# A step between two layers with tokens on the partitions, first sums of squares on TensorE, and last rows set among spilled pairs

## The chip, the cores and the metric

The kernel runs on one core of one Trainium2 chip. The metric is the time of one execution in microseconds on the device. The kernel before has a median of 2876.93 us over 3 runs (2876.14 to 2879.42). One execution was profiled; it took 2871.39 us by the same clock, and its trace spans 2869.6 us.

## The reference

A trunk of two layers works on two streams of 256 tokens with 1024 features each: the latent `x` and a context `ctx`. Each layer is a group of four token mixers and then an expert network (PEER). Cut to what matters here:

```python
for l in range(DEPTH):                     # DEPTH = 2
    last = l == DEPTH - 1
    sh1, sc1, g1, sh2, sc2, g2 = _modulation(c, w_mod[l], b_mod[l])       # silu(c) @ w_mod + b_mod
    sh1c, sc1c, g1c, sh2c, sc2c, g2c = _modulation(c_ctx, w_mod[l], b_mod[l])
    hx = _rmsnorm(x, norm_mix[l]) * (1 + sc1) + sh1
    hc = _rmsnorm(ctx, norm_mix[l]) * (1 + sc1c) + sh1c
    y, yc = _mixers(hx, hc, w_in[l], ..., not last)     # one input projection, four mixers, w_out
    x = x + g1 * y
    hx2 = _rmsnorm(x, norm_ffn[l]) * (1 + sc2) + sh2
    if last:
        x = x + g2 * _peer(hx2, ...)
    else:
        ctx = ctx + g1c * yc
        hc2 = _rmsnorm(ctx, norm_ffn[l]) * (1 + sc2c) + sh2c
        f = _peer(jnp.concatenate([hc2, hx2], axis=1), ...)
        ctx = ctx + g2c * f[:, :C]                      # C = 256 tokens of context
        x = x + g2 * f[:, C:]
return _rmsnorm(x, final_norm)
```

`_peer` takes for each token and each of 8 heads the 16 best of 128 x 128 experts, and adds `gate * gelu(h . u[i]) * v[i]` over them. `_rmsnorm` divides by the root of the mean square over the 1024 features.

## The kernel before

**Layout.** The streams lie in one tile `xT` of 128 partitions x 8 x 512: feature k*128+p of a token on partition p, the tokens on the free axis, first the 256 of the context (stream s = 0), then the 256 of x (s = 1). Features on the partitions are what a matmul wants that sums over features; a sum of squares over features then takes a matmul with a matrix of ones, and a gate per feature is a scalar per partition.

**Arithmetic.** Each fp32 operand of a large matmul is split into a high and a low part of a faster type (`hH` and `hL`, `wH` and `wL`, `vH` and `vL`, `ah` and `al`), and three products are summed: high x high, high x low, low x high. The splits run on ACT (high, L211) and on DVE or POOL (low, L215).

**Order of the work.** (1) The start: silu of c, its rows of 128 x 512 by four groups of matmuls (L284, copied by ACT at L286), the two modulation rows of layer 0, half by matrix products on PE (`mod_first`, L311 and L315), half by dot products on DVE (`mod_rows`, L296), and meanwhile the sums of squares of both streams: ACT squares each of 8 feature blocks (L339, L342), POOL adds them (L344), and two matmuls with ones bring the sum to all partitions (L347, L348). `norm_mod` (L360 to L364) turns xT into `hH` and `hL`. (2) The mixers of layer 0: the input projection in slabs of 128 columns (L224), then the mixers. (3) PEER of layer 0: scores over all experts (u phase), then the values (v phase) in pairs of expert blocks: `pa`, three token tiles of PSUM accumulators, gathers `ah`/`al` x `vH`/`vL` (L1312). Tile 0, the first 128 tokens of the context, is instead summed from single gathered rows by DVE and POOL, in the generator `gathered`, which runs in between the pairs; at its end it transposes its sum back (L1072) and adds it to xT (`resid`, L375). (4) The step between the layers: after the last pair the accumulators are copied (L1335, L1337), transposed to features (L1344), gated and added to xT (L375), squared and summed (`sumsq`), and `norm_mod` gives the `hH` and `hL` of layer 1. (5) Mixers of layer 1, (6) PEER of layer 1 for x alone. Its v phase begins with pairs whose scores are computed there and then, and ends with pairs that were spilled to memory earlier and are read back (`ga`). `finish_rows` (L1356, L1364) prepares what the end needs: the gate and the final gain as rows on all partitions, and x with tokens on the partitions; it stands ahead of the v phase. `finish` (L1378 to L1394) then gates, adds, normalises and stores.

**What sets the order.** In the v phase of layer 0 and in the step behind it the order on PE, DVE, ACT and POOL is that of the code. Elsewhere a scheduler orders the instructions within what the tiles' buffers allow. PSUM tiles with the name `S` go round in a small ring, so a group of transposes waits until the copy out of an earlier one is done.

Of the kernel before, what the change touches and what calls it, by code (L numbers as in the profile page):

```python
# [9 lines left out]
F32 = mybir.dt.float32  # L10
# [11 lines left out]
P = 128  # L22
D = 1024
KT = 8
# [47 lines left out]
GATED = (1, 4)  # L72
VALUES = (5, 0)
# [111 lines left out]
class Kernel:  # L185
# [149 lines left out]
    def sumsq(self, k, c, psp, tag, eng=None):  # L335
# [9 lines left out]
        else:  # L345
            ps = self.t(psp, [P, T], tag=tag)
            nc.tensor.matmul(ps[:, c], self.ones, self.sqsum[:, c], start=True, stop=False)  # L347
            nc.tensor.matmul(ps[:, c], self.ones, sq[:, c], start=False, stop=True)  # L348
            self.rstd_from(self.rstd[:, c], ps[:, c], D)
# [304 lines left out]
    def mixers(self, l, modt, tick=None, pre=()):  # L654
# [5 lines left out]
        with ExitStack() as es:  # L660
            fp = es.enter_context(tc.tile_pool(name=f"fp{l}", bufs=1))
            psp = es.enter_context(tc.tile_pool(name=f"ps{l}", bufs=2, space=PSUM))
            hx = self.norm_mod(0, modt, 1, 0, fp)
# [3 lines left out]
            def feat(name, ct, lo):  # L667
                w = slabs.pop(0) if slabs else self.in_slab(l, name, ct)
                b.nfeat += 1
                ps = self.proj(w, hx, lo, psp, last and b.nfeat <= 3)  # L670
                if tick:
                    ticks(1)
                return ps
# [182 lines left out]
            for piece in ORDERS[l]:  # L856
                name, _, d = piece.partition(":")
                locals()[name](*map(int, d))
            yT = (self.t(None, [P, KT, T], F32R, tag="hH"), self.t(None, [P, KT, T], F32R, tag="hL"))
# [134 lines left out]
    def gathered(self, l, gate, h2, idx, gates, gp, mods, modt):  # L994
# [74 lines left out]
        for q in range(2):  # L1069
            pt = self.t(self.gps[0], [P, 4, P], tag=self.gps[1])  # L1070
            for k in range(4):
                nc.tensor.transpose(pt[:, k, :], acc[:, (q * 4 + k) * P:(q * 4 + k) * P + P], self.ident)  # L1072
            for k in range(4):
                self.resid(q * 4 + k, pt[:, k, :], gate, 0, slice(0, P))
            yield

    def peer(self, l, mods, todo=()):
# [10 lines left out]
        with ExitStack() as es:  # L1088
# [122 lines left out]
            with ExitStack() as e2:  # L1211
# [11 lines left out]
                if last:  # L1223
                    rows = self.finish_rows(vp, psp, modt[5])
# [56 lines left out]
                for g, i in enumerate(order):  # L1281
                    ah, al, vs = b.ah, b.al, b.vs
                    left = len(order) - 1 - g
                    if left:
# [43 lines left out]
                self.norm_start()  # L1328
                f = {}
                for tau in taus:  # L1330
                    f[tau] = self.t(vp, [P, D], tag="vH", bufs=4)
                    for h in range(2):
                        dst = f[tau][:, h * 512:h * 512 + 512]
                        if h:
                            V.tensor_copy(dst, pacc[tau, h])  # L1335
                        else:
                            S.activation(dst, pacc[tau, h], AF.Copy)  # L1337
                for s, c in self.halves(dl):
                    for d in range(KT):
                        ps = self.t(psp, [P, T], tag="S")  # L1340
# [170 lines left out]
```

## Time and profile before

| | us |
|---|---|
| median of 3 runs | 2876.93 (2876.14 to 2879.42) |
| the profiled execution, its own time | 2871.39 |
| its span in the trace | 2869.6 |
| PE busy | 2705.5 (94% of the span) |
| DVE busy | 2048.3 (71%) |
| ACT busy | 1149.8 (40%) |
| POOL busy | 1098.5 (38%) |

PE is TensorE's matmul side, DVE VectorE, ACT ScalarE, POOL GpSimd, SP the engine that issues the DMAs. A share over the whole span is a mean over stages with different limits, so each stage is looked at by itself. Starts are in microseconds from the start of the span. The times of a sum are those of the profiled execution; 1.8 us of it lie outside the span.

### The profile page before, as it was taken

Reading aid. Unit: us, or ns where it says so; the run is one execution under the profiler, and the core shown is the slowest. Engines: PE = TensorE matmul, PEld = TensorE weight load, DVE = VectorE, ACT = ScalarE, POOL = GpSimd, SP = SyncE. Lnnn points to the kernel's source line nnn. Section 1 sums busy time; section 2 is a strip of 40 time slices with the busy share of each in tenths; the row PEclk is TensorE's granted clock in tenths of the full one; section 3 lists DMA queues with packets and bytes.
Section 4 is the critical chain, followed back from the end, with each engine's and each line's share of the span. In section 5 each row is a group of like instructions: output and inputs, shape, how many; then the busy total and the mean of one; then the engine's idle time right before and its main releaser. Section 6 shows DMA issues by size and latency. Waiting matters only on the chain. (4 is left out here: it accounts for less than half of the span.)

```text
span 2869.6 us, 41545 instructions
## 1 busy us (share of the span) xinstructions
PE 2705.5 (94%) x15778; PEld 2398.3 (84%) x15778; DVE 2048.3 (71%) x3608; ACT 1149.8 (40%) x1752; POOL 1098.5 (38%) x651
## 2 busy tenths in 40 slices
PE   7899999889999999999999998899889999999998
PEld 4677888789998888888888877688889998998776
DVE  6785778999677788898888877847982404555665
ACT  4433433235533333333333334434344545444443
POOL 3631134455145344344343313425656574440000
PEclk9898999989999999999999998999999999999999
DMA  6223423257789899999999952324557776667785
GB/s 238 67 81 111 128 89 121 93 171 269 282 294 321 304 327 329 323 340 338 346 328 342 378 195 67 110 89 149 158 183 240 234 257 205 213 207 255 268 273 186
DMA packets 265784, 639.25 MB, mean 223 GB/s; under 512 B 19184, under 2 KB 136688, under 8 KB 262768
## 3 DMA queue, kind: packets, MB, share of 16 engines
q1 hardware_dynamic: 228720, 502.36, 52.2%
q0 software_dynamic: 36864, 134.23, 12.8%
q8 instruction: 124, 2.03, 0.3%
q14 instruction: 76, 0.62, 0.1%
HBM read 574.39 MB, written 62.13 MB: 222 GB/s over the span
## 5 line engine op out<-in xcount | busy, mean ns | idle before, releaser
L215 POOL TENSOR_TENSOR wL<-wraw,wH 128x1024 fp32r<-128x1024 f32 x228 | 572.6, 2514 | 694.4 <-ACT wH L211 541.8
L224 PE MATMUL S<-hH,wL 128*128 128x384 f32 (+1 forms) x2048 | 606.4, 314 | 21.0 <-POOL wL L215 11.3
L224 PE MATMUL S<-hH,wH 128*128 128x384 f32 (+1 forms) x2048 | 606.3, 314 | 5.8 <-ACT wH L211 4.2
L211 ACT ACTIVATE wH<-wraw 128x1024 fp32r<-128x1024 f32 x320 | 337.1, 1054 | 335.0 <-DMA wraw<-in_uT_dram 297.9
L224 PEld LDWEIGHTS S<-hH,wL 128*128 128x128 f32 x2048 | 393.6, 192 | 32.1 <-DVE wL L215 17.9
L1312 PE MATMUL pa<-vH,al 128*128 128x512 f32 x1280 | 397.7, 391 | 8.3 <-DVE al L1263 7.9
L224 PEld LDWEIGHTS S<-hH,wH 128*128 128x128 f32 x2048 | 393.8, 192 | 11.2 <-ACT wH L211 6.8
L1312 PE MATMUL pa<-vL,ah 128*128 128x512 f32 x1280 | 396.9, 391 | 2.5 <-DVE vL L215 2.3
L1312 PE MATMUL pa<-vH,ah 128*128 128x512 f32 x1280 | 395.6, 390 | 2.0 <-ACT ah L1259 1.2
L215 DVE TENSOR_TENSOR vL<-wraw,vH 128x1024 fp32r<-128x1024 f32 x256 | 305.7, 1223 | 68.1 <-ACT vH L211 66.8
L224 PE MATMUL S<-hL,wH 128*128 128x384 f32 (+1 forms) x2048 | 347.5, 310 | 0.0
L211 ACT ACTIVATE vH<-wraw 128x1024 fp32r<-128x1024 f32 x256 | 263.9, 1054 | 188.6 <-PE pa L1312 158.0
L224 PEld LDWEIGHTS S<-hL,wH 128*128 128x128 f32 x2048 | 311.5, 190 | 0.0
L1013 POOL DMA_INDIRECT row<-in_v_dram,idx x128 | 190.4, 1487 | 293.4 <-DVE tok L1064 266.2
L1312 PEld LDWEIGHTS pa<-vH,al 128*128 128x128 f32 x1280 | 238.5, 188 | 65.2 <-DVE al L1263 16.4
L1013 POOL DMA_INDIRECT row<-in_u_dram,idx x128 | 182.2, 1424 | 279.0 <-DVE score L1046 237.5
L1312 PEld LDWEIGHTS pa<-vL,ah 128*128 128x128 f32 x1280 | 239.0, 188 | 57.2 <-DVE vL L215 8.0
L1312 PEld LDWEIGHTS pa<-vH,ah 128*128 128x128 f32 x1280 | 238.1, 188 | 48.1 <-ACT ah L1259 1.6
L1109 ACT ACTIVATE ga<-S 128x384 f32<-128x384 f32 (+1 forms) x256 | 111.1, 435 | 385.4 <-PE S L224 384.3
L224 PE MATMUL mm<-hH,wH 128*128 128x256 f32 (+1 forms) x776 | 256.1, 349 | 9.4 <-ACT hH L362 2.9
L224 PE MATMUL mm<-hH,wL 128*128 128x256 f32 (+1 forms) x776 | 251.4, 343 | 5.6 <-DVE wL L215 5.3
L215 DVE TENSOR_TENSOR wL<-wraw,wH 128x1024 fp32r<-128x1024 f32 x128 | 156.1, 1227 | 118.4 <-ACT wH L211 112.8
(340 smaller groups left out, 4048.8 us busy)
## 6 DMA issues: line engine op xcount, KB each, us to landing
wraw<-in_uT_dram SPq DMA_DIRECT2D x256, 512.0 KB
wraw<-in_v_dram SPq DMA_DIRECT2D x256, 512.0 KB
gd<-gst SPq DMA_DIRECT2D x20, 2048.0 KB
wraw<-in_w_in_dram SPq DMA_DIRECT2D x52, 512.0 KB
gt<-gd SPq DMA_DIRECT2D x32, 768.0 KB
row<-in_w_modT_dram SPq DMA_DIRECT2D x48, 512.0 KB
wraw<-in_w_modT_dram SPq DMA_DIRECT2D x32, 512.0 KB
wraw<-in_w_q_dram SPq DMA_DIRECT2D x32, 512.0 KB
```

Source lines behind the costliest of these rows:

```text
L211: nc.scalar.activation(h, w, AF.Copy)
L215: e.tensor_tensor(lo, w, h.bitcast(F32), op=ALU.subtract)
L224: nc.tensor.matmul(ps, x, y, start=start and m == 0, stop=stop and m == len(seq) - 1, skip_group_check=skip)
L1013: Gp.indirect_dma_start(out=x, out_offset=None, in_=rows[n], in_offset=bass.IndirectOffsetOnAxis(ap=idx[:, k:k + 1], axis=0))
L1109: self.gelu = S.activation(ga[:, e, :], ps, AF.Gelu_apprx_tanh)
L1312: nc.tensor.matmul(pacc[tau, h], (ah, ah, al)[m][:, e, tau * P:(tau + 1) * P], vs[e][m == 1][:, h * 512:h * 512 + 512], start=g == 0 and e ...
```

## The change

It has three parts.

**The step between the layers.** In the v phase of layer 0, six pairs before its end, a new function `token_rows` turns xT to tokens on the partitions (32 transposes, 8 copies) and makes the gates as rows on all partitions (16 matmuls with the identity, 4 copies). `gathered` no longer transposes its sum; it leaves it in `acc0`. After the last pair, `hand_over` gates and adds tile by tile with tokens on the partitions (`normed`), where the sum of squares of a token is a sum along the free axis; the normalised tile is transposed to features, modulated and split (`features`): first the tiles 0, 2, 3, then the features of x, then tile 1, then the features of the context. In layer 1 the first two slabs are projected for the columns of x first and then for those of the context. After the piece `d_out` of the mixers of layer 1 x is transposed back to features (16 transposes, 8 copies).

**The first sums of squares.** `sumsq_pe` takes the place of `sumsq`: 8 matmuls with ones, one for each feature block, sum the squares in PSUM; POOL's 6 adds are gone.

**The last step's rows.** `finish_rows` of layer 1 is called six pairs before the end of the v phase instead of ahead of it.

```diff
+ROWSAT = 6
...
+    def sumsq_pe(self, k, c, ps):
+
+        sq = self.t(None, [P, T], tag="t2")
+        self.nc.scalar.activation(sq[:, c], self.xT[:, k, c], AF.Square)
+        self.nc.tensor.matmul(ps[:, c], self.ones, sq[:, c], start=k == 0, stop=k == KT - 1)
+        if k == KT - 1:
             self.rstd_from(self.rstd[:, c], ps[:, c], D)
...
-            hx = self.norm_mod(0, modt, 1, 0, fp)
+            hx = self.hx if last else self.norm_mod(0, modt, 1, 0, fp)
...
             def feat(name, ct, lo):
+                if last and b.nfeat < 2:
+                    x = [(hx[0][:, k, C:], hx[1][:, k, C:]) for k in range(KT)]
+                    if b.nfeat == 0:
+                        b.two = [(self.in_slab(l, name, e), self.t(psp, [P, T], tag="mm", bufs=self.nmm)) for e in range(2)]
+                        for w, ps in b.two:
+                            self.mm3(ps[:, C:], [(w[0][:, k, :], w[1][:, k, :]) for k in range(KT)], x)
+                    w, ps = b.two[b.nfeat]
+                    b.nfeat += 1
+                    self.mm3(ps[:, :C], [(w[0][:, k, :], w[1][:, k, :]) for k in range(KT)],
+                             [(hx[0][:, k, :C], hx[1][:, k, :C]) for k in range(KT)])
...
+                if last and name == "d_out":
+                    for k in range(KT):
+                        ps = self.t(psp, [P, T], tag="tr")
+                        for c in (C, C + P):
+                            nc.tensor.transpose(ps[:, c:c + P], self.xT[:, k, c:c + P], self.ident)
+                        S.activation(self.xT[:, k, C:], ps[:, C:], AF.Copy)
...
-        for q in range(2):
-            pt = self.t(self.gps[0], [P, 4, P], tag=self.gps[1])
-            for k in range(4):
-                nc.tensor.transpose(pt[:, k, :], acc[:, (q * 4 + k) * P:(q * 4 + k) * P + P], self.ident)
-            for k in range(4):
-                self.resid(q * 4 + k, pt[:, k, :], gate, 0, slice(0, P))
-            yield
+        self.acc0 = acc
...
-                if last:
-                    rows = self.finish_rows(vp, psp, modt[5])
...
+                    if left == ROWSAT:
+                        rows = self.finish_rows(vp, psp, modt[5]) if last else self.token_rows(vp, psp, modt[5])
...
-                self.norm_start()
-                f = {}
-                for tau in taus:
...
+                self.hand_over(vp, pvp, taus, pacc, rows, mods[1])
+
+    def token_rows(self, pool, psp, gate):
+
+        nc = self.nc
+        for k in range(KT):
+            ps = self.t(psp, [P, 4, P], tag="S")
+            for tt in range(4):
+                nc.tensor.transpose(ps[:, tt, :], self.xT[:, k, tt * P:tt * P + P], self.ident)
+            nc.scalar.activation(self.xT[:, k, :], ps.rearrange("p t n -> p (t n)"), AF.Copy)
+        g = [[self.t(pool, [P, T], tag=tag, bufs=1) for tag in tags] for tags in (("grow0", "rstd"), ("grow1", "grow2"))]
+        for s in range(2):
+            for q in range(2):
+                ps = self.t(psp, [P, 4, P], tag="S")
+                for k in range(4):
+                    nc.tensor.matmul(ps[:, k, :], gate[q][:, k, s:s + 1].to_broadcast([P, P]), self.ident, start=True, stop=True)
+                nc.scalar.activation(g[s][q], ps.rearrange("p k n -> p (k n)"), AF.Copy)
+        return g
+
+    def hand_over(self, pool, pvp, taus, pacc, gates, modt):
...
+        def normed(tt, src, tag):
+            y = self.xT[:, :, tt * P:tt * P + P]
+            w[tt] = self.t(pool, [P, D], F32R, tag=tag, bufs=4).bitcast(F32)
+            wv = w[tt].rearrange("p (k n) -> p k n", n=P)
+            ss = self.t(pool, [P, 2], tag="ss")
+            for h in range(2):
+                c, q = slice(h * 512, h * 512 + 512), slice(h * 4, h * 4 + 4)
+                V.tensor_tensor(w[tt][:, c], src(h), gates[int(tt >= 2)][h], op=ALU.mult)
+                V.tensor_tensor(y[:, q], y[:, q], wv[:, q], op=ALU.add)
+                S.activation(wv[:, q], y[:, q], AF.Square, accum_out=ss[:, h:h + 1])
+            r = self.t(pool, [P, 1], tag="rs")
+            V.tensor_tensor(r, ss[:, 0:1], ss[:, 1:2], op=ALU.add)
+            self.rstd_from(r, r, D)
+            S.activation(wv[:, :4], y[:, :4], AF.Copy, scale=r)
+            V.tensor_scalar(wv[:, 4:], y[:, 4:], r, None, op0=ALU.mult)
+
+        def features(s, tags):
+            c = slice(s * C, s * C + C)
+            for k in range(KT):
+                if k % 2 == 0:
+                    ps = self.t(pvp, [P, 2, C], tag=tags[k // 2], bufs=1)
+                x = ps[:, k % 2, :]
+                for e in range(2):
+                    nc.tensor.transpose(x[:, e * P:e * P + P], w[s * 2 + e][:, k * P:k * P + P], self.ident)
+                sc, sh = [modt[m][k // 4][:, k % 4, s:s + 1] for m in (1, 0)]
+                if k % 2:
+                    S.activation(x, x, AF.Identity, scale=sc, bias=sh)
+                else:
+                    V.tensor_scalar(x, x, sc, sh, op0=ALU.mult, op1=ALU.add)
+                S.activation(H[:, k, c], x, AF.Copy)
+                V.tensor_tensor(L[:, k, c], x, H[:, k, c].bitcast(F32), op=ALU.subtract)
+
+        normed(0, lambda h: self.acc0[:, h * 512:h * 512 + 512], "vL")
+        for tau, tag in zip(taus[:2], ("vH", "vL")):
+            normed(tau + 1, lambda h: pacc[tau, h], tag)
+        features(1, [f"pa{tau}{h}" for tau in taus[:2] for h in range(2)])
+        normed(1, lambda h: pacc[0, h], "vH")
+        features(0, ["pa00", "pa01"] + [f"pa{taus[1]}{h}" for h in range(2)])
+        self.hx = H, L
...
-                    self.norm_start()
+                    self.rstd = self.t(None, [P, T], tag="rstd")
+                    acc = self.t(wmp, [P, T], tag="ss", bufs=1)
...
-                            self.sumsq(k, slice(0, T), wmp, "mm", nc.gpsimd)
+                            self.sumsq_pe(k, slice(0, T), acc)
```

Where the instructions stand now is shown at three places, on PE.

The first place is the end of the step, where layer 1's first projection starts. Before, the last transposes of the accumulators and the two sums stand ahead of the first projection matmul (`mm` is its PSUM tile, `hH` x `wH`):

```order
L1344 MATMUL S_14499<-small_59,vH_14404 128x128
L1344 MATMUL S_14505<-small_59,vH_14404 128x128
L347 MATMUL S_14510<-t_2801_14396,small_59 128x256
L348 MATMUL S_14510<-t_2836_14508,small_59 128x256
L224 MATMUL mm_14625<-hH_14553,wH_14621 128x256
L224 MATMUL mm_14625<-hH_14553,wL_14622 128x256
```

In the changed kernel (its own line numbers; `vL_14456` and `vH_14542` are the normalised tiles 0 and 1, the two of the context, and `small` holds the identity):

```order
L1401 MATMUL pa_2829_14531<-small_59,vH_14470 128x128
L1401 MATMUL pa_2829_14531<-small_59,vL_14484 128x128
L1401 MATMUL pa_2833_14556<-small_59,vL_14456 128x128
L1401 MATMUL pa_2833_14556<-small_59,vH_14542 128x128
...
L1401 MATMUL pa_2836_14589<-small_59,vL_14456 128x128
L1401 MATMUL pa_2836_14589<-small_59,vH_14542 128x128
L225 MATMUL mm_14656<-hH_14454,wH_14652 128x256
L225 MATMUL mm_14656<-hH_14454,wL_14653 128x256
```

All 16 transposes of the context, which read tile 1, stand ahead of the first projection matmul, which reads columns of x alone.

The second place is the v phase of layer 0, the pair with six left. Before, its matmuls followed those of the pair ahead without a break:

```order
L1312 MATMUL pa_1331_6761<-vL_13889,ah_13897 128x512
L1312 MATMUL pa_1332_6762<-vL_13889,ah_13897 128x512
L1312 MATMUL pa_1331_6761<-vH_13888,al_13898 128x512
L1312 MATMUL pa_1332_6762<-vH_13888,al_13898 128x512
L1312 MATMUL pa_1327_6757<-vH_13946,ah_13959 128x512
L1312 MATMUL pa_1328_6758<-vH_13946,ah_13959 128x512
```

In the changed kernel `token_rows` stands between two pairs (the last two of its eight groups of transposes are shown, and its four groups of gates):

```order
L1358 MATMUL S_14032<-small_59,xT_65 128x128 x4
L1358 MATMUL S_14038<-small_59,xT_65 128x128 x4
L1365 MATMUL S_14048<-small_59,mod_19_87 128x128 x4
L1365 MATMUL S_14054<-small_59,mod_20_88 128x128 x4
L1365 MATMUL S_14060<-small_59,mod_19_87 128x128 x4
L1365 MATMUL S_14066<-small_59,mod_20_88 128x128 x4
L1334 MATMUL pa_1327_6757<-vH_13946,ah_13959 128x512
L1334 MATMUL pa_1328_6758<-vH_13946,ah_13959 128x512
```

Twelve groups of four stand there, ahead of the next pair's first matmul.

The third place is `finish_rows` of layer 1. Before, between two score products (`S`, L224) at the start of the v phase:

```order
L224 MATMUL S_21358<-hL_16807,wH_21327 128x256 x8
L1356 MATMUL S_21400<-small_59,mod_31_99 128x128 x4
L1356 MATMUL S_21406<-small_59 128x128 x4
L1356 MATMUL S_21412<-small_59,mod_32_100 128x128 x4
L1356 MATMUL S_21418<-small_59 128x128 x4
L1364 MATMUL S_21425<-small_59,xT_65 128x128 x4
L1364 MATMUL S_21431<-small_59,xT_65 128x128 x4
L1364 MATMUL S_21437<-small_59,xT_65 128x128 x4
L1364 MATMUL S_21443<-small_59,xT_65 128x128 x4
L224 MATMUL S_21468<-hH_16806,wH_21451 128x256
```

In the changed kernel, among the products of the spilled pairs:

```order
L1334 MATMUL pa_4016_21460<-vH_25179,al_25188 128x512
L1426 MATMUL S_25254<-small_59,mod_31_99 128x128 x4
L1426 MATMUL S_25260<-small_59 128x128 x4
L1426 MATMUL S_25266<-small_59,mod_32_100 128x128 x4
L1426 MATMUL S_25272<-small_59 128x128 x4
L1434 MATMUL S_25279<-small_59,xT_65 128x128 x4
L1334 MATMUL pa_4013_21457<-vH_25218,ah_25230 128x512
L1434 MATMUL S_25285<-small_59,xT_65 128x128 x4
L1434 MATMUL S_25291<-small_59,xT_65 128x128 x4
L1334 MATMUL pa_4014_21458<-vH_25218,ah_25230 128x512
L1434 MATMUL S_25297<-small_59,xT_65 128x128 x4
L1334 MATMUL pa_4013_21457<-vL_25219,ah_25230 128x512
```

The same eight groups are there; the last three lie between products of the next pair.

## Rows read from the trace of the kernel before

**Rows 1.** Windows: length, busy PE, PEld, DVE, ACT, POOL; clock, DMA share, GB/s.

```profile
15.00:20.00 5.00, 0.00 (x0) 0.00 (x0) 4.93 (x5) 0.63 (x1) 4.84 (x3) 0.51 1.05 396
...
1600.00:1680.00 80.00, 80.00 (x355) 66.24 (x354) 66.94 (x65) 29.68 (x30) 19.07 (x12) 1.00 0.97 341
...
1712.00:1736.00 24.00, 11.18 (x32) 5.22 (x30) 17.33 (x45) 11.85 (x29) 1.36 (x1) 0.56 0.08 22
...
1860.00:1880.00 20.00, 19.80 (x128) 17.40 (x127) 9.46 (x25) 2.22 (x4) 1.15 (x1) 0.88 0.08 27
...
2374.00:2377.00 3.00, 3.00 (x14) 3.00 (x15) 0.00 (x0) 1.32 (x3) 1.74 (x1) 0.50 0.94 344
...
2380.00:2420.00 40.00, 39.93 (x268) 37.05 (x269) 18.39 (x13) 19.62 (x28) 18.97 (x8) 1.00 0.62 194
```

**Rows 2.** Timeline of the start: start, us, engine, line, tiles, count [idle before, releaser].

```profile
8.60 11.43 POOL L344 TENSOR_TENSOR t<-t,t 128x512 f32<-128x512 f32 x6 [4.35 <-ACT t L342]
...
18.95 2.16 DVE L296 CUSTOM_DVE_ANT_0 modj<-wmod,silu_rows,small 128x1024 bf16<-128x1024 f32 x1
...
22.48 1.28 DVE L296 CUSTOM_DVE_ANT_0 modj<-wmod,silu_rows,small 128x1024 bf16<-128x1024 f32 x1
...
20.08 2.08 PE L347 MATMUL mm<-t,small 128*128 128x512 f32 x2 [9.35 <-POOL t L344]
...
23.79 7.79 PE L311 MATMUL mm<-wf,silu_c 128*2 128x512 f32 x16
...
45.37 0.50 PE L224 MATMUL mm<-hH,wH 128*128 128x512 f32 x1 [0.25 <-DVE mod L317]
...
20.59 3.75 SPq L305 DMA_DIRECT2D wf<-in_w_first_dram  x2
```

**Rows 3.** Timeline of the step between the layers.

```profile
1701.18 2.98 DVE L1263 TENSOR_TENSOR al<-ga,ah 128x768 fp32r<-128x768 f32 x1 [0.36 <-ACT ah L1259]
...
1711.16 0.62 PE L1312 MATMUL pa<-vH,al 128*128 128x512 f32 x2
...
1724.95 0.91 ACT L362 ACTIVATE hH<-big,mod 128x256 fp32r<-128x256 f32 x2
...
1735.79 0.58 PE L224 MATMUL mm<-hH,wH 128*128 128x256 f32 x1 [0.56 <-ACT rstd L328]
...
1737.02 0.41 PE L224 MATMUL mm<-hH,wL 128*128 128x256 f32 x1
```

**Rows 4.** Timeline of `finish` at the end of layer 1, second tile.

```profile
2859.19 0.68 DVE L1378 TENSOR_TENSOR fo<-pa,grow 128x512 f32<-128x512 f32 x1
2859.91 0.69 DVE L1379 TENSOR_TENSOR xtok<-xtok,fo 128x512 f32<-128x512 f32 x1
...
2864.68 0.15 DVE L1386 TENSOR_TENSOR rs<-ss 128x1 f32<-128x1 f32 x1
2865.43 0.49 DVE L1394 TENSOR_SCALAR fo<-xtok,rs 128x512 f32<-128x512 f32 x1 [0.60 <-ACT rs L329]
...
2863.32 0.63 ACT L1381 ACTIVATE fo<-xtok 128x512 f32<-128x512 f32 x1 [1.96 <-DVE xtok L1379]
```

**Rows 5.** Timeline: transposes and rows by matmul, with their copies.

```profile
1682.81 0.60 PE L1072 MATMUL S<-small,tok 128*128 128x128 f32 x4
...
2369.70 1.05 PE L1356 MATMUL S<-small,mod 128*128 128x128 f32 x8
...
2373.86 2.08 PE L1356 MATMUL S<-small,mod 128*128 128x128 f32 x8 [2.21 <-ACT grow L1357]
...
2380.56 0.39 PE L224 MATMUL S<-hH,wH 128*128 128x256 f32 x1
...
2367.70 8.04 POOL L215 TENSOR_TENSOR wL<-wraw,wH 128x1024 fp32r<-128x1024 f32 x3 [4.18 <-ACT wH L211]
...
2379.42 1.09 ACT L1365 ACTIVATE xtok<-S 128x512 f32<-128x512 f32 x2
```

**Rows 6.** Waits of PE from 2600 to 2853 us: us in total, times, longest.

```profile
PE pa L1312 <- DVE al L1263: 6.9, 12, 1.0
```

More of the change, by code (lines that the diff above doesn't have):

```diff
@@ L348, in sumsq @@
             nc.tensor.matmul(ps[:, c], self.ones, sq[:, c], start=False, stop=True)
+            self.rstd_from(self.rstd[:, c], ps[:, c], D)
+    def sumsq_pe(self, k, c, ps):
[3 more added lines that the diff above has]
+        if k == KT - 1:
             self.rstd_from(self.rstd[:, c], ps[:, c], D)
@@ L662, in mixers @@
             psp = es.enter_context(tc.tile_pool(name=f"ps{l}", bufs=2, space=PSUM))
-            hx = self.norm_mod(0, modt, 1, 0, fp)
+            hx = self.hx if last else self.norm_mod(0, modt, 1, 0, fp)
             slabs = list(pre)
             def feat(name, ct, lo):
+                if last and b.nfeat < 2:
[8 more added lines that the diff above has]
+                             [(hx[0][:, k, :C], hx[1][:, k, :C]) for k in range(KT)])
+                    if tick:
+                        ticks(1)
+                    return ps
                 w = slabs.pop(0) if slabs else self.in_slab(l, name, ct)
@@ L1327, in peer @@
                     return
-                self.norm_start()
-                f = {}
-                for tau in taus:
[L1331 to L1340, printed above, removed]
-                        for tau in sorted(taus):
-                            at = dl + tau * P
-                            if c.start <= at < c.stop:
-                                nc.tensor.transpose(ps[:, at:at + P], f[tau][:, d * P:(d + 1) * P], self.ident)
-                        self.resid(d, ps, modt[5], s, c)
-                        self.sumsq(d, slice(s * C, s * C + C), psp, "S")
+                self.hand_over(vp, pvp, taus, pacc, rows, mods[1])
@@ new lines, in hand_over @@
+    def hand_over(self, pool, pvp, taus, pacc, gates, modt):
+        nc = self.nc
+        V, S = nc.vector, nc.scalar
+        H = self.t(None, [P, KT, T], F32R, tag="hH")
+        L = self.t(None, [P, KT, T], F32R, tag="hL")
+        w = {}
+        def normed(tt, src, tag):
[35 more added lines that the diff above has]
+        self.hx = H, L
```

## The prediction

> **What bounds the kernel now.** I read the table of busy shares first (DVE 71%, PE nearly full) and then asked, with windows, where PE isn't full, since only there can an edit off PE gain, and in the full stretches each instruction added to PE costs its own length. [...] In the v phase of layer 0 PE works 80.00 of 80 us, in the mixers of layer 1 19.80 of 20, and behind the start of layer 1's v phase 39.93 of 40 [rows 1]. At the start PE does nothing from 15 to 20 us, where DVE (4.93 of 5) and POOL (4.84) are full [rows 1]. [...] The timeline of each stretch then shows what the next matmul waits for.
>
> **Part 1, the first sums of squares.** Before, six adds of POOL hold the squares: 8.60 + 11.43 us = 20.03, and PE's sum starts at 20.08, its last releaser POOL L344 [rows 2]. `mod_first` follows at 23.79, and the first projection starts at 45.37 [rows 2]. Beside those adds the dot products on DVE take 2.16 us each, without them 1.28 [rows 2]. After: eight ones-matmuls of 128x512. The two of before took 2.08 at the lower clock [rows 2], so about 1.0 each while PE is warm, and PE comes warm from the silu rows. Eight follow their squares on ACT and on PE end near 17.4 instead of 23.8, so this chain gives 6.4. The weights of `mod_first` may be later than that: SP issues its next weight tiles only at 20.59 [rows 2], and by the order it waits there for the landing of this product's own two, so they may land as late as that and the first product may start anywhere between 17.4 and about 20.5 without a wait of its own coming last. That is a gain of 3.3 to 6.4, plus up to 0.7 if the first product, 7.79 long at a clock still rising [rows 2], runs warm throughout: 4 to 7. DVE, with 8 dot products at about 1.32 from start to start, is free near 21.4 instead of 25.1 and isn't last. I take the middle, **-5.5**. Everything behind shifts with it, PE being the limit from the first projection on.
>
> **Part 2, the step between the layers.** Before, the last product of the pairs ends at 1711.16 + 0.62 = 1711.8, the first projection starts at 1735.79: 24.0 us [rows 3]. After, DVE starts with tile 0 once its last `al` is done, 1701.18 + 2.98 = 1704.2 [rows 3], while PE still multiplies. A tile's chain has its rows in `finish`: two halves of a product (0.72 from start to start) and an add (0.69), 2.8; the square on ACT 0.63 and its sum about 0.2; from the add of the two sums to the scaling 0.75, the scaling 0.49 [rows 4]. Together 4.8 from tile to tile. Three tiles end at 1718.5. The features of x: per pair of blocks the modulation, two copies and two subtractions on DVE and ACT, each about 0.45 (the 256-column copies of L362 take 0.91 for two [rows 3]), some 2.0 a pair in the order written, 8.1 in all: 1726.6. Tile 1, 4.8: 1731.4, and about 0.8 until its ACT half is scaled.
>
> Then comes what the order on PE shows: the sixteen transposes of the context stand ahead of the first projection of x, so x's features, ready at 1727, wait for the context. Four transposes end 0.35 after their start when warm, the next product starting then (1682.81, 0.60 long with its drain [rows 5]), twice that when cold: 1.8 to 3.4 for sixteen. The first projection so starts between 1734 and 1735.6, against 1735.79. The first matmuls behind are cold in both (0.41 long at 1737.02 [rows 3]). I take **-1.5**. Both ends: if DVE's last `al`, 2.98 long for 768 columns, took what the 0.68 of a 512-column product [rows 4] makes by width, 1.0 (an estimate), 2 more are gained, and 0.5 more if the tiles overlap, so -4; if each tile costs 1 us more than in `finish` (four wide operands now pass through the strided xT, which no row shows), +3.
>
> What pays for it stands on a full PE. `token_rows`: eight groups of four transposes, each with a copy on ACT of 128x512 at 1.09 for two [rows 5], and a ring of few PSUM tiles: about 0.6 a group, 4.8. Four groups of gates: the first like it in `finish_rows` ends 0.9 to 1.05 after its start [rows 5], 3.8 for four. Together 8.6. The lower bound is PE's own time without a wait for copies, 8 x 0.35 + 4 x 0.9 = 6.4. The upper one is the rate at which `finish_rows` went: eight groups from 2369.70 to 2380.56, 10.86 [rows 5], so twelve take 16.3. There the second pair of gates was held 2.21 by the copy on ACT and ran at a clock of 0.50 (2.08 long instead of 1.05) [rows 1, 5]. In the v phase of layer 0 ACT works 29.68 of 80 us [rows 1], and its copies stand contiguous there, so I take the value near the lower end, 8.6. The transposes that fall away (L1072, two groups, 0.42 each with gaps) give 0.85 back: **+7.75**.
>
> The transposes of x back in layer 1: sixteen at 0.09 to 0.12, **+2**, on a PE busy 19.80 of 20 us [rows 1]; 1.5 if they fit with no gap, 4.9 if each pair waits for its copy (8 x 0.6).
>
> **Part 3, the last step's rows.** Removed: 10.86 from 2369.70 to 2380.56 [rows 5]. Not all comes back: the next score product reads a low part that POOL makes at 2367.70 + 8.04/3 = 2370.4, 0.7 behind the place, and the following ones go at POOL's rate of 2.68 a tile [rows 5], so 1 to 2 us of waits that the rows hid come out: 8 to 10.9, I take 9.4. Behind it PE is full (39.93 of 40) with a DMA share of 0.62 [rows 1], so the transfers can follow. Added: the same eight groups among the spilled pairs, ACT being free there: 4 x 0.95 + 4 x 0.55 = 6.0, at most 10.9 as before. PE has 6.9 us of waits for `al` in 253 us there [rows 6], about 1 in what is left of the pairs after the place, and that may absorb 1: 4.9. Net **-4.5**, from -2 to -6.5.
>
> **Sum.** -5.5 - 1.5 + 7.75 + 2 - 4.5 = -1.75 against the profiled execution's 2871.39: 2869.6. The median is 5.5 above the profiled execution, so about **2875** for the median after. A change within 0.2%, 5.75 us, can't be told from none.
>
> [...] In the stretch from 2374 to 2377, with PE busy 3.00 of 3.00 after a wait of 2.21, the granted clock was 0.50 [rows 1, 5]; it is a row with gates, not with transposes alone. [...]
>
> **Rivals.**
> First, the gains reach their bounds: no DMA holds `mod_first` (-7), the start of layer 1's v phase gives back all 10.9 (-6), and the short `al` starts the step earlier (-3.5). With 7.75 and 2 that is -6.75: 2870. For it speaks that all three are waits whose releasers are seen to go; against it the late issue at 20.59 and the 2.68 a tile on POOL. Add a `token_rows` at its lower bound and it is 2868.
>
> Second, slower: the clock falls inside `token_rows`. PE alternates there with ACT's copies for some 5 us; from the point at which the level falls before the gates, four groups of gates cost 1.9 instead of 0.95, +3.8, and the first products of the next pair go at half rate for as long as it lasts, some 2 to 3 us lost; the transposes back in layer 1 the same way +1.5. So the sum is -1.75 + 7.8 = +6: 2883. For it: clock 0.50 in `finish_rows` [rows 1]. Against it: there PE first waited 2.21 us in one piece, while here no gap is longer than a copy.
>
> Third, the start is limited by its weights: DMA is busy throughout (396 GB/s from 15 to 20 us, share 1.05 [rows 1]), the products wait for tiles and part 1 gives 1 to 2: +2, 2879, still no change that can be told.
>
> **How the numbers follow.** Forecast 0.40 (own range 2871 to 2879), first rival 0.27, second 0.23, third 0.10. Faster: nearly all of the first rival (0.25) and the low end of the forecast (0.07), 0.32. Slower: nearly all of the second (0.22) and a little of the third (0.02), 0.24. Within 0.2%: what is left, 0.44. The range reaches from the first rival with a `token_rows` at its lower bound, 2867, to the second with the step gaining nothing, 2885.
>
> **What would show it.** At the start: no POOL adds, dot products of 1.28 throughout, `mod_first` from 17 to 21 and the first projection near 40; if it stands near 44, the weights were last. In the v phase of layer 0: a stretch of 8 to 9 us with twelve groups at clock 1.00; 0.50 there speaks for the second rival. From the last product of the pairs to the first projection 22 to 23 us instead of 24.0, with transposes of the context last before it and DVE the busiest; if it is over 24, a tile costs more than in `finish`. In layer 1's v phase no gap over 2 us at its start, and some 6 us between two pairs near the end. The prediction is wrong if any one of the three parts is off by more than 5 us.

## The result and the profile after

The changed kernel takes 2895.87 us (median of 4 runs, 2893.09 to 2897.70), the kernel before 2878.12 beside it: ratio 1.0063, 95% interval 1.0038 to 1.0088. Run again on another chip the ratio was 1.0125 (1.0102 to 1.0148). It is slower, by 18 to 29 us, where 2 us faster was forecast with a range of 2867 to 2885. The profiled execution has a span of 2892.8 us, 23.2 more than before.

Since both kernels split each pair of the v phases' gated scores once on ACT (`ah`, 64 pairs in layer 0, then 64 in layer 1), the start of the same `ah` in two traces tells where a lead or a lag arises. The lag is that start minus the start of the same `ah` in the trace of before. The table has the change of the lag between marks, in us (worked out from those starts; negative is gained):

| stretch | changed | before, part 2 alone | before, part 3 alone | pause kept | own ring |
|---|---|---|---|---|---|
| start to `ah` 0 | -6.6 | -0.8 | -1.2 | -5.9 | -4.8 |
| `ah` 0 to 57: v phase of layer 0 | -8.7 | -4.2 | -3.1 | 0.1 | -8.2 |
| 57 to 58: `token_rows` | 10.6 | 10.6 | 0.0 | 10.6 | 10.6 |
| 58 to 63: the pairs behind it, L1072's groups gone | -3.4 | -3.4 | 0.0 | -3.4 | -3.4 |
| 63 to 65: step, mixers, start of layer 1's v phase | 9.0 | 19.9 | -2.8 | 19.0 | 7.0 |
| 65 to 81: its scored pairs | **20.4** | -0.7 | 8.6 | 0.7 | -2.2 |
| 81 to 122: spilled pairs | -3.4 | -0.8 | -2.7 | -1.0 | 2.5 |
| 122 to 127: last rows | 5.0 | 0.4 | 5.1 | 5.1 | 5.1 |

The kernels of the last four columns are the experiments `a_alone`, `c_alone`, `pause` and `ownv` below. The first two rows differ between executions of one kernel: the changed kernel, run once more (`after_again`), has 9.4 and -1.5 in them instead of -6.6 and -8.7 (last section). The fifth row holds the mixers of layer 1, where a kernel that is unchanged there can lose 5.5 us (`c_alone`: its lag is -4.3 at the first projection of layer 1 and 1.2 at the copies of layer 1's scores, `ga<-S` on ACT, from 2173 to 2325 us in the trace of before, where the lags stand still). The other rows repeat: the run once more has 10.6, -3.4, 18.2, -2.1 and 5.1.

**The start.** Timeline of the changed kernel, PE:

```profile
12.37 6.17 PE L356 MATMUL ss<-t,small 128*128 128x512 f32 x14
18.47 7.03 PE L312 MATMUL mm<-wf,silu_c 128*2 128x512 f32 x16
...
39.29 0.50 PE L225 MATMUL mm<-hH,wH 128*128 128x512 f32 x1 [0.26 <-DVE mod L318]
```

The first projection starts at 39.29, 6.1 us ahead of 45.37 [rows 2]. `mod_first` (L312) starts at 18.47, right behind the sums of squares (L356): its weights weren't last.

**`token_rows`.** Timeline, PE, and windows (length, busy PE, PEld (weight loads), DVE, ACT, POOL, clock, DMA share, GB/s):

```profile
1636.96 1.03 PE L1358 MATMUL S<-small,xT 128*128 128x128 f32 x8
1638.25 1.14 PE L1358 MATMUL S<-small,xT 128*128 128x128 f32 x8 [0.25 <-ACT xT L1359]
...
1642.28 3.90 PE L1365 MATMUL S<-small,mod 128*128 128x128 f32 x32 [0.20 <-ACT xT L1359]
1645.93 0.70 PE L1334 MATMUL pa<-vH,ah 128*128 128x512 f32 x2
```

```profile
1636.00:1642.00 6.00, 5.35 (x37) 4.03 (x36) 0.68 (x1) 3.63 (x7) 2.42 (x2) 1.00 1.05 332
1642.00:1646.00 4.00, 3.80 (x34) 3.72 (x33) 0.00 (x0) 2.51 (x5) 0.00 (x0) 1.00 0.09 33
```

It takes 1645.93 - 1636.96 = 9.0 us at clock 1.00.

**The step.** Timeline, DVE (the tiles 0, 2 and 3, the features of x, tile 1, the end of the features of the context), ACT and PE:

```profile
1696.10 0.68 DVE L1385 TENSOR_TENSOR vL<-tok,grow 128x512 f32<-128x512 f32 x1
...
1700.78 0.68 DVE L1385 TENSOR_TENSOR vH<-pa,grow 128x512 f32<-128x512 f32 x1
...
1705.47 0.68 DVE L1385 TENSOR_TENSOR vL<-pa,grow 128x512 f32<-128x512 f32 x1
...
1709.75 0.48 DVE L1392 TENSOR_SCALAR vL<-xT,rs 128x512 f32<-128x512 f32 x1 [0.60 <-ACT rs L330]
1711.04 0.55 DVE L1406 TENSOR_SCALAR pa<-pa,mod,mod 128x256 f32<-128x256 f32 x1 [0.80 <-PE pa L1401]
1712.04 0.42 DVE L1408 TENSOR_TENSOR hL<-pa,hH 128x256 fp32r<-128x256 f32 x1 [0.45 <-ACT hH L1407]
1714.24 0.42 DVE L1408 TENSOR_TENSOR hL<-pa,hH 128x256 fp32r<-128x256 f32 x1 [1.77 <-ACT hH L1407]
1714.58 0.54 DVE L1406 TENSOR_SCALAR pa<-pa,mod,mod 128x256 f32<-128x256 f32 x1
...
1724.82 0.42 DVE L1408 TENSOR_TENSOR hL<-pa,hH 128x256 fp32r<-128x256 f32 x1 [1.77 <-ACT hH L1407]
...
1729.44 0.49 DVE L1392 TENSOR_SCALAR vH<-xT,rs 128x512 f32<-128x512 f32 x1 [0.60 <-ACT rs L330]
...
1744.50 0.42 DVE L1408 TENSOR_TENSOR hL<-pa,hH 128x256 fp32r<-128x256 f32 x1 [1.77 <-ACT hH L1407]
...
1713.25 0.54 ACT L1404 ACTIVATE pa<-pa,mod,mod 128x256 f32<-128x256 f32 x1 [1.24 <-PE pa L1401]
...
1703.21 0.61 PE L1334 MATMUL pa<-vH,al 128*128 128x512 f32 x2
...
1712.52 0.48 PE L1401 MATMUL pa<-small,vH 128*128 128x128 f32 x1 [1.52 <-DVE hL L1408]
...
1743.06 0.42 PE L1401 MATMUL pa<-small,vH 128*128 128x128 f32 x1
1744.98 0.58 PE L225 MATMUL mm<-hH,wH 128*128 128x256 f32 x1 [1.50 <-DVE hL L1408]
```

A tile takes 1705.47 - 1700.78 = 4.7, as forecast. But a pair of feature blocks takes 1714.58 - 1711.04 = 3.5, not 2.0: PE's transposes of the second block (1712.52) wait for `hL` of the first. And the first projection, which reads columns of x alone, starts at 1744.98, 1.50 behind the last transpose of the context: its releaser is the context's last `hL` (1744.50 + 0.42). So it waits for all of the context's features, and not for their transposes only. The last product of the pairs ends at 1703.21 + 0.61 = 1703.8, so the step is 41.2 us where it was 24.0 [rows 3]; in every kernel with part 2 as written it is 41.2, in every one without it 24.0.

**The scored pairs of layer 1's v phase.** Timeline of the changed kernel, one pair: ACT, DVE, POOL and SP (SPq is the queue that issues the DMAs), then the two `vL` of it apart (count, ns least/median/most), and the waits of PE from 2420 to 2580 us (us in total, times, longest):

```profile
2496.41 1.06 ACT L212 ACTIVATE wH<-wraw 128x1024 fp32r<-128x1024 f32 x1 [7.33 <-DMA wraw<-in_uT_dram]
2497.38 0.62 ACT L1279 ACTIVATE ah<-ga 128x512 fp32r<-128x512 f32 x1
...
2498.02 2.49 DVE L1283 TENSOR_TENSOR al<-ga,ah 128x512 fp32r<-128x512 f32 x1 [4.75 <-ACT ah L1279]
2500.43 4.56 DVE L216 TENSOR_TENSOR vL<-wraw,vH 128x1024 fp32r<-128x1024 f32 x2
...
2501.18 2.72 POOL L216 TENSOR_TENSOR wL<-wraw,wH 128x1024 fp32r<-128x1024 f32 x1 [1.22 <-ACT wH L212]
...
2505.02 0.81 SPq L398 DMA_DIRECT2D wraw<-in_uT_dram  x2
...
2509.15 1.06 ACT L212 ACTIVATE wH<-wraw 128x1024 fp32r<-128x1024 f32 x1 [7.77 <-DMA wraw<-in_uT_dram]
...
L216 DVE TENSOR_TENSOR vL<-wraw,vH x2: 1214/2317/3420, 2500.4 to 2501.6; 128x1024 fp32r<-128x1024 f32 x2
...
PE pa L1334 <- DVE al L1283: 9.9, 10, 1.3
```

The same of the kernel before, DVE, POOL, SP and ACT, and at the end its `al` from 2600 to 2850 us, among the spilled pairs:

```profile
2487.06 2.49 DVE L1263 TENSOR_TENSOR al<-ga,ah 128x512 fp32r<-128x512 f32 x1 [3.50 <-ACT ah L1259]
2489.48 2.35 DVE L215 TENSOR_TENSOR vL<-wraw,vH 128x1024 fp32r<-128x1024 f32 x2
...
2498.15 2.49 DVE L1263 TENSOR_TENSOR al<-ga,ah 128x512 fp32r<-128x512 f32 x1 [3.37 <-ACT ah L1259]
...
2491.82 2.40 POOL L215 TENSOR_TENSOR wL<-wraw,wH 128x1024 fp32r<-128x1024 f32 x1 [2.82 <-ACT wH L211]
...
2491.85 2.73 SPq L389 DMA_DIRECT2D wraw<-in_uT_dram  x2
...
2496.53 1.06 ACT L211 ACTIVATE wH<-wraw 128x1024 fp32r<-128x1024 f32 x1 [2.85 <-DMA wraw<-in_uT_dram]
2497.50 0.61 ACT L1259 ACTIVATE ah<-ga 128x512 fp32r<-128x512 f32 x1
...
L1263 DVE TENSOR_TENSOR al<-ga,ah x44: 681/684/686, 2600.5 to 2847.2; 128x512 fp32r<-128x512 f32 x44
```

Read as a ring, from start to start: the two `vL` are done (2500.43 + 4.56 = 2504.99), which frees a raw tile (a tile that a load lands in); SP issues the next u tile (2505.02); it lands 4.1 later; its high part on ACT takes 1.0; `ah` stands behind it on ACT, 0.65; `al` takes 2.4, the two `vL` 4.55, and round again: 12.7 us in this pair, 12.59 in the mean, with no work of PE in it. PE waits for `al`. In the kernel before the two `vL` take 2.35, since POOL's split of `wL` starts (2491.82) when they are done, and the u tile lands 4.7 after its issue (2491.85 to 2496.53): the ring is 4.7 + 1.0 + 0.65 + 2.4 + 2.35 = 11.1. PE's work is 11.2 a pair (the kernels with the ring opened, below), so there PE is the limit. My reading of how the slow ring lasts, which no run tried by itself: once PE is ahead of the ring, ACT gets its scores early, makes the second `wH` early, and POOL's split (2501.18) falls on the `vL`. Of the two, the one that had started takes 1.21, the one behind it 3.42. So a `vL` took 3.42 beside `wL` and 1.2 without; why, no run shows. The same shows in both rings: `al` takes 2.49 beside POOL's other split of the pair, and 0.68 among the spilled pairs, where there is none. Those 1.8 us of either ring no run tried to take out.

### The profile page after: what moved, and what is told of

Its sections match the earlier page's. It is cut to its first block, busy times and chain, and to the rows that moved or that the text cites. A ratio compares the mean times of both kernels' runs of the same rounds, so it can differ in the third digit from the quotient of the medians.

```text
span 2892.8 us, 41729 instructions
## 1 busy us (share of the span) xinstructions
PE 2709.9 (94%) x15862; PEld 2400.9 (83%) x15862; DVE 2065.7 (71%) x3585; ACT 1160.5 (40%) x1785; POOL 1089.0 (38%) x645
## 3 DMA queue, kind: packets, MB, share of 16 engines
q0 software_dynamic: 36864, 134.23, 12.6%
## 4 chain that ended last, share of the span: by engine, by line
PE 38%; DVE 24%; DMA 18%; issue 11%; ACT 5%; POOL 3%; DVEq 0%; ACTq 0%; SPq 0%; POOLq 0%
PE S L225 11%; DMA wraw<-in_uT_dram 10%; PE mm L225 10%; DVE vL L216 7%; PE pa L1334 5%; PE G L1219 4%; DMA ga<-spd 4%; ACT ah L1279 1%; ACT wH L212 1%; DVE ga L1276 1%; DMA row<-in_u_dram,idx 1%; DVE wL L216 1%; PE o L631 1%; DMA wraw<-in_v_dram 1%; DVE eq L967 1%
## 5 line engine op out<-in xcount | busy, mean ns | idle before, releaser
L225 PEld LDWEIGHTS S<-hH,wL 128*128 128x128 f32 x2048 | 392.5, 192 | 27.1 <-POOL wL L216 12.9
L216 DVE TENSOR_TENSOR vL<-wraw,vH 128x1024 fp32r<-128x1024 f32 x256 | 340.2, 1359 | 83.7 <-ACT vH L212 83.0
L1283 DVE TENSOR_TENSOR al<-ga,ah 128x768 fp32r<-128x768 f32 (+1 forms) x128 | 137.3, 1073 | 142.0 <-ACT ah L1279 142.0
```

Of the source, the lines that this page charges most:

```text
L216: e.tensor_tensor(lo, w, h.bitcast(F32), op=ALU.subtract)
L225: nc.tensor.matmul(ps, x, y, start=start and m == 0, stop=stop and m == len(seq) - 1, skip_group_check=skip)
L1283: V.tensor_tensor(b.al, b.gated, b.ah.bitcast(F32), op=ALU.subtract)
```

## The experiments

Executions of one kernel on one chip lie up to 25 us to either side of their median, so medians tell parts of the sum apart badly; the stages above that repeat tell them apart well. Both are given.

**One part at a time.** Part 1 alone (the kernel before with `sumsq_pe`), part 3 alone, part 2 alone, each by the hunks of the diff above.

> The kernel before with the first sums of squares on TensorE and nothing else. In the changed kernel the first projection started 6.1 us earlier (39.29 against 45.37). Theory: the whole kernel moves by that, -6 us, plus what the v phase of layer 0 makes of it (in the changed kernel the lead grew there from 6.6 to 15.2 us before token_rows; if that comes from the earlier start, -14 here; if it comes from part 2, -6). Rival: the lead is lost later in a wait that doesn't depend on the start, 0.

> The kernel before with finish_rows moved among the last spilled pairs and nothing else. Theory: without the pause of 10.9 us at the start of layer 1's v phase the 16 or so scored pairs run as a ring (low parts vL done, load of the next u tile, its high part, ah, al, vL) at 12.4 us a pair instead of 11.2, about +20; with -8 at the start and +6 near the end, +15 to +20 in all. Rival: the slow pairs come from parts 1 or 2 (another phase on arrival); then this kernel has 11.2 us a pair and is faster by 2 to 4.

> The changed kernel with parts 1 and 3 undone: only the step between the layers. Theory: token_rows +9, the two groups that fall away -1 to -2, the step 41 us from the last product to the first projection instead of 24, so +17, the transposes back +2: +24 to +28 with scored pairs at 11.2 us. If the lead in layer 0's v phase came from part 2: 8 less. Rival: the 41 us step comes in part from where part 1 left DVE and POOL; then the step is near 30 here.

Part 1: ratio 0.9982 (0.9945 to 1.0018), unclear alone. In its profile the lead is 5.2 us at `ah` 0 and 0.4 at `ah` 57, so the rival that it is lost later isn't refuted; in layer 1 the step is 24.0 us as before, and the last of the scored pairs take up to 13.1, 3.5 us lost in all, although the pause that `finish_rows` makes ahead of them is there. Part 3: 1.0047 (1.0013 to 1.0081), slower, though by less than the 15 to 20 us expected. Its start of layer 1's v phase gains 8.8 (lag 1.2 to -7.6 at the copies of the scores); then its first interval between two `ah` is 12.6 us, the next ten are 11.1 to 11.6, and from the twelfth on they are over 12: +8.6 in all. So the slow ring comes without parts 1 and 2, though not at once. Its profiled execution, 2875.35, is one of its fastest (median 2889.08), so others may lose more there. Part 2: 1.0138 (1.0083 to 1.0193), the step 41.2, pairs at 11.3: 10.6 - 3.4 + 19.9 = +27.1 from `ah` 57 to 65. The rival that part 1 lengthens the step fell.

**The pause kept.** In the kernel before `finish_rows` made a pause of 10.9 us on PE ahead of the scored pairs. The changed kernel with a second, unused call where it stood before:

```diff
+                if last:
+                    self.finish_rows(vp, psp, modt[5])
                 order = list(range(nsp, NE, 2)) + list(range(0, nsp, 2))
```

> The changed kernel with finish_rows called at both places, the first call's results not used. Theory (the pause lets the loads get ahead): scored pairs at 11.2 us again, so against the changed kernel +9 at the start and -20 in the pairs: about 11 faster than the changed kernel, near 2885. Rival (the place of finish_rows in the late order, or the earlier arrival, is what slows the pairs): pairs stay at 12.4 and it is 8 to 10 slower than the changed kernel, near 2905.

The scored pairs are 0.7 us in all off the kernel before, and PE is full. Its ratio is 1.0092 (1.0059 to 1.0124); the changed kernel ran on other chips, so only the stages compare. Windows of 160 us of these pairs, the changed kernel's and then this one's:

```profile
2420.00:2580.00 160.00, 150.09 (x940) 133.14 (x940) 97.97 (x52) 64.81 (x91) 66.19 (x26) 1.00 0.58 187
```

```profile
2420.00:2580.00 160.00, 160.00 (x1036) 146.68 (x1035) 82.35 (x57) 76.46 (x100) 67.85 (x29) 1.00 0.65 209
```

PE goes from 150.09 to 160.00 of 160, and DVE does more pairs in less busy time, 82.35 instead of 97.97. So the 10.9 us that stood there did work. What it did is not shown by itself; that the loads got ahead in it is likely, with a DMA share of 0.94 inside it [rows 1]. It doesn't rule the slow ring out for good, as the last pairs of part 1 alone show.

**The ring opened.** v tiles of layer 1 in a ring of their own, in the changed kernel and in before with part 1:

```diff
-b.w = [self.t(None, [P, KT, P], tag="wraw").rearrange("p k n -> p (k n)") for e in range(2)]
+b.w = [(self.t(vp, [P, KT, P], tag="wv", bufs=4) if last else self.t(None, [P, KT, P], tag="wraw"))
+       .rearrange("p k n -> p (k n)") for e in range(2)]
```

> The changed kernel, with the v tiles of layer 1's v phase loaded into a ring of their own (4 tiles of a pool that has room there) instead of sharing the four raw tiles with the u tiles. Theory (a closed ring: vL done frees the raw tile, u load 4.1, high part 1.0, ah 0.65, al 2.4, two vL 4.55, together 12.6 a pair, longer than PE's 11.2): the u load no longer waits for vL, PE is the limit again, 11.2 to 11.4 a pair, some 18 us less than the changed kernel. Rival (the DMA queue or ACT's order behind the u tile makes the 12.6): pairs stay at 12.4 to 12.6, no gain.

> The kernel before with part 1 (first sums on TensorE) and the own ring for the v tiles of layer 1's v phase. Theory: -6 from part 1, and pairs of 11.2 or less also where the kernel before falls into the ring of 12.4; so at least as fast as part 1 alone, 2860 to 2868, and less spread between runs. Rival: the kernel before never falls into the slow ring and part 1's lead is lost: 2873 to 2879.

In both the pairs take 11.21 us in the mean (`ah` 66 to 81), without the pause in the first: 12.59 in the changed kernel, 11.32 in before. The rival is refuted: what closed the ring is that u tiles and v tiles share the raw tiles. In the first each `vL` takes 1.23 again, so it doesn't tell whether the sharing alone, without the long `vL`, would have cost anything. The times: 1.0050 (1.0026 to 1.0074), and 0.9991 (0.9972 to 1.0009), no change that can be told (for this second one 2860 to 2868 was expected, and 2871.10 came).

**Transposes ahead, and banks apart.** First the transposes of both blocks are written ahead of the work on either, in the changed kernel and with the own ring:

```diff
                 if k % 2 == 0:
                     ps = self.t(pvp, [P, 2, C], tag=tags[k // 2], bufs=1)
+                    for j in range(2):
+                        for e in range(2):
+                            at = (k + j) * P
+                            nc.tensor.transpose(ps[:, j, e * P:e * P + P], w[s * 2 + e][:, at:at + P], self.ident)
                 x = ps[:, k % 2, :]
-                for e in range(2):
-                    nc.tensor.transpose(x[:, e * P:e * P + P], w[s * 2 + e][:, k * P:k * P + P], self.ident)
```

> The changed kernel, with both transposes pairs of a PSUM tile in features written ahead of the work on either half. Theory (the second half's transposes wait for the first half's last reader, hL, because both lie in one PSUM tile): a pair of blocks falls from 3.53 to about 2.0 us, eight pairs give 12 us, the step from the last product to the first projection 41 to about 29 us. Rival (DVE's and ACT's alternation itself takes 3.5 a pair): nothing changes in the step.

> The changed kernel with both repairs, the own ring and the transposes ahead. Theory: both gains add, -12 and -18: near 2866, so no slower than the kernel before. Rival (the repairs hit the same wait): about -15.

The step fell to 36.1 in both, 5 us where 12 were expected. Timeline of the first (ACT, DVE, then PE at the end of the step):

```profile
1735.23 0.54 ACT L1406 ACTIVATE pa<-pa,mod,mod 128x256 f32<-128x256 f32 x1 [0.49 <-DVE hL L1410]
...
1733.77 0.55 DVE L1408 TENSOR_SCALAR pa<-pa,mod,mod 128x256 f32<-128x256 f32 x1 [1.23 <-PE pa L1402]
...
1736.56 0.54 DVE L1408 TENSOR_SCALAR pa<-pa,mod,mod 128x256 f32<-128x256 f32 x1
...
1752.99 0.42 PE L1402 MATMUL pa<-small,vH 128*128 128x128 f32 x1
1762.25 0.55 PE L225 MATMUL mm<-hH,wH 128*128 128x256 f32 x1 [8.84 <-DVE hL L1410]
```

Now ACT's work on the second block waits for `hL` of the first: the two still take turns at one tile, 2.8 a pair. And the context's transposes are done 8.84 us before the first projection, which still waits for the context's last `hL`: the order on PE isn't what holds it. What ties it to the context's `hL`, the tile `hL` that holds both streams or the PSUM tile that this subtraction is the last to read, no run tells. The ratios are 1.0093 (1.0066 to 1.0120) without the own ring and 1.0042 (1.0021 to 1.0063) with it; with both repairs a time near 2866 was expected, and 2886.04 came. Then each block got a PSUM tile of its own (its expectation calls it a bank), and the two were worked on side by side, with the own ring:

```diff
-            for k in range(KT):
+            for q in range(0, KT, 2):
+                xs = [self.t(pvp, [P, 2, C], tag=tags[k % 4], bufs=1)[:, 0, :] for k in (q, q + 1)]
...
+                for k, x in zip((q, q + 1), xs):
+                    S.activation(H[:, k, c], x, AF.Copy)
+                for k, x in zip((q, q + 1), xs):
+                    V.tensor_tensor(L[:, k, c], x, H[:, k, c].bitcast(F32), op=ALU.subtract)
```

> The changed kernel with the own ring for v tiles, and in features each feature block in a PSUM bank of its own, the two of a pair worked on side by side (modulation, copy, subtraction each for both). Theory (with the transposes ahead a pair still took 2.78, because ACT's modulation of the second half waited for the first half's hL, which lies in the same PSUM tile): about 2.0 a pair, so 16 us for both streams instead of 28, the step 29 us instead of 41.2, and in all 6 to 8 less than with the transposes alone ahead. Rival (ACT and DVE are full at 2.8 a pair): step stays at 36.

> The changed kernel once more, beside the two below on one chip. Theory: 0.6 to 1.0% slower than before, step 41.2 us, scored pairs of layer 1's v phase at 12.4 to 12.6 us if the ring closes behind the earlier start of the phase (always, as the pause is gone). Rival (the slow ring was chance in the first profile): pairs at 11.2 to 11.5 here, and the time 18 us lower than in the first profile's stages.

> The kernel before with part 1, part 3 and the own ring, without part 2. Theory: -6 from the start, -2 to -3 from the last rows' place once the ring isn't closed (-8 at the start of the phase, +6 near the end), 11.2 a pair: 8 to 10 faster than before, near 2868, the fastest of all. Rival: the lead of the start is lost in layer 0 and the time is that of before.

Timeline of the kernel with banks apart, DVE:

```profile
1728.32 0.55 DVE L1407 TENSOR_SCALAR pa<-pa,mod,mod 128x256 f32<-128x256 f32 x1
1729.32 0.76 DVE L1411 TENSOR_TENSOR hL<-pa,hH 128x256 fp32r<-128x256 f32 x2 [0.45 <-ACT hH L1409]
1729.99 0.55 DVE L1407 TENSOR_SCALAR pa<-pa,mod,mod 128x256 f32<-128x256 f32 x1
```

1.7 a pair, the step 26.9 us. The order of the work on ACT changed together with the tiles (its modulation now stands ahead of the first copy), so how much each of the two gave isn't told apart.

The last three kernels ran on one chip: the changed kernel 1.0125 (step 41.2, pairs 12.4 again, so the slow ring wasn't chance), with both repairs 1.0001 (0.9984 to 1.0017), and parts 1 and 3 with the own ring, without part 2, **0.9973 (0.9954 to 0.9992)**: 2870.87 against 2879.94, a little faster than the kernel before. In that last one the lag goes from -4.0 at the copies of layer 1's scores to -8.3 at the end; in the same kernel without part 3 (`b_ownv`) from 4.6 to -0.3. So with the own ring part 3 brings nothing that can be told. In its profile all of the lead, 8.6 us, is there at `ah` 57; how much of it is part 1's is not shown, since its clock at the start was the best of all (1.00 from 205 to 265 us, last section).

## Why the prediction was wrong

**Part 1 was right at the place that it changes**: 6.1 us at the first projection against 5.5, and about 5 at `ah` 0 once the clock is allowed for (last section). That "everything behind shifts with it, PE being the limit from the first projection on" isn't shown: the row read for layer 0's v phase (80.00 of 80) is from its end, and in the stretches of 100 us from 780 to 1580 PE is busy between 94.85 and 99.46 of 100 in the kernel before. In the three kernels with part 1 and the old step, the lead shrinks by 4.9, 4.6 and 4.3 from `ah` 0 to 57, and in two of them 0.4 and 0.6 are left; why isn't known.

**Part 2, the cost on PE, was about right**: `token_rows` 9.0 against 8.6, and with the pairs behind it 10.6 - 3.4 = 7.2 against 7.75. The second rival, a falling clock, didn't come: 1.00 in both windows of `token_rows`, over its 5.3 us of transposes (1636.96 to 1642.28) and over the gates behind them (the forecast's "warm" and "cold" are granted clocks of 1.00 and 0.50). The +2 for the transposes of x back don't show either: the lag is 9.2 at the first projection of layer 1 and 9.1 at the copies of its scores.

**Part 2, the step, is the first step that failed**, by 18.7 us (41.2 where 22.5 was forecast), in two terms of its sum. The first term: "The features of x: per pair ... some 2.0 a pair in the order written, 8.1 in all" took 15.0 (1710.23 to 1725.24), 6.9 more. The sum took two blocks of a pair as side by side, though they lie in one PSUM tile, and work of different engines on one tile was put in sequence: first PE's transposes (1.52 idle ahead of 1712.52, released by `hL`), then, when these stood ahead, ACT's modulation (0.49 idle ahead of 1735.23, released by `hL`). The second term: for the context the sum had only 0.8 and its sixteen transposes, "1.8 to 3.4 for sixteen"; from the end of tile 1 to the first projection it took 15.1 (1729.93 to 1744.98), 12 more. The transposes of one pair wait for the work on the pair's first block, so the context's modulation, copies and subtractions all stand on the path; and even with the transposes ahead the first projection waited for the last of them, 8.84 us. With a tile for each block the same two stretches took 7.9 and 7.9: the features of x then take what was forecast, those of the context 5 more, and the step, 26.9, is still no better than 24.0. "-1.5" could not have come. The tiles themselves were right: 14.1 for three against 14.3, and 4.7 against 4.8.

**Part 3 is the second**: "Behind it PE is full (39.93 of 40) with a DMA share of 0.62 [rows 1], so the transfers can follow." The gain at the start came (lag 9.1 to 1.1 at `ah` 65, 8 us, where 9.4 was forecast), the cost at the end came (5.0, forecast 4.9). But the share of a resource isn't the length of a ring: before, the ring of load, splits and release was 11.1 against PE's 11.2, so PE was full by 0.1 us a pair. Without the pause the ring was 12.6, and 16 pairs cost 20.4 us. Neither range nor rivals had this; what was to show the start of layer 1's v phase, "no gap over 2 us at its start", was so (the longest wait is 1.3 us), and the loss came behind it.

In sum, from `ah` 57 on: 10.6 - 3.4 + 9.0 + 20.4 - 3.4 + 5.0 = 38.2, less the 15.3 of lead before: 23. Of that lead part 1 explains 5 to 6; the rest differs between executions. (The lower end of the range is worked out as 2868 in the first rival and given as 2867; that changes nothing here.)

## What to carry to other kernels

A stall on a full engine may be what keeps a loop behind it full: before taking it out, add up the ring of load, split, use and release by its durations, and compare it with the full engine's work a turn (here 11.1 against 11.2 with the stall, 12.6 without), instead of reading a DMA share (0.62 here). Two pieces of work on one PSUM tile went in a row here, 3.5 us a pair where the sum had 2.0; with a tile for each, and ACT's order changed, 1.7 came. So sum them in a row unless the order's waits say otherwise. And an instruction that reads only some columns may still be released by work on the others: here, with the transposes ahead, PE stood idle for 8.84 us before the first projection, which reads columns of x, until the context's last `hL`, though which tile tied it to that isn't told. And where one execution differs from the next by more than the change, compare the same instruction's start stage by stage.

## What the runs showed that was not expected

Much of the spread in the first row of the table comes from TensorE's clock in the mixers of layer 0 (0.63, 0.89 and 1.00 in the rows below). Windows of two executions of the same changed kernel, the first profile and then the repeat, and of `bc_ownv`:

```profile
230.00:235.00 5.00, 5.00 (x21) 4.59 (x20) 3.90 (x6) 2.14 (x3) 1.55 (x1) 0.50 0.09 32
...
205.00:265.00 60.00, 59.43 (x348) 50.31 (x348) 35.46 (x76) 20.94 (x52) 9.27 (x6) 0.89 0.39 128
```

```profile
215.00:220.00 5.00, 5.00 (x19) 4.10 (x18) 1.49 (x3) 0.60 (x1) 0.00 (x0) 0.50 0.18 53
...
250.00:255.00 5.00, 5.00 (x22) 4.61 (x21) 0.99 (x4) 0.00 (x0) 0.00 (x0) 0.50 0.66 210
...
205.00:265.00 60.00, 59.50 (x230) 48.12 (x229) 32.77 (x69) 10.61 (x23) 6.73 (x5) 0.63 0.34 107
```

```profile
205.00:265.00 60.00, 58.29 (x380) 48.80 (x379) 38.61 (x80) 25.23 (x61) 9.57 (x6) 1.00 0.40 129
```

PE counts as busy 5.00 of 5 in each of the short windows, yet the granted clock is 0.50, in one execution from about 226 to 239 us, in the other from about 212 to 256, and in `bc_ownv` never between 205 and 265. A mean clock of 0.89 in these 60 us costs 60 x (1 - 0.89) = 6.6 us, one of 0.63 22.2 (estimates from the rows, PE being busy nearly throughout). Taken off the start of `ah` 0 (774.66, 790.61 and 768.40), they leave 768.1, 768.4 and 768.4. Done the same way for all thirteen traces, the ten with part 1 lie between 766.9 and 768.4, the three without it between 772.1 and 773.5: so the spread of the first row is this clock, and part 1 is worth about 5 us at `ah` 0. What starts the fall wasn't tried. From 205 to 210 us PE is busy 4.50 of 5 in both executions that have it, but 4.51 in `bc_ownv` too, which hasn't.
